# Second modulation moved from the LRU tiles into the S5 input and transform stages, and two LRU steps moved from VectorE to ScalarE

## The chip, the core and the metric

The kernel runs on one core of a Trainium2 chip. The metric is the device time of one execution in microseconds (us). Before the change it was 2331.53 us, the median of three runs (2328.48, 2331.53 and 2334.17).

The engines are called as the profile calls them: PE (TensorE, matrix multiply), DVE (VectorE), ACT (ScalarE), POOL (GpSimd) and SP (SyncE, which here issues nearly all transfers). Each runs its own queue strictly in order; a waiting instruction holds up everything behind it on its engine.

## What is computed

One layer of a hybrid backbone on 256 context tokens and 1024 latent tokens, width 1024, all in float32. Cut to what the change touches:

```python
m_lat = cond_lat @ w_mod[i] + b_mod[i]          # 1024 x 6144: six vectors of 1024
sh1l, sc1l, gt1l, sh2l, sc2l, gt2l = split(m_lat, 6)
z = modulate(rms_norm(h, norm1), sh1, sc1) @ w_in
xa, ga, zb, uc, zg = split(z)                   # LRU, its gate, RWKV, S5, merge gates

# LRU, each of two directions
xc = conv_centred(xa, conv_w, conv_b)           # bias + 4 taps
gate_r = sigmoid(xc @ w_a + b_a); gate_i = sigmoid(xc @ w_x + b_x)
log_a = -8 * gate_r * softplus(-lam)
a = exp(log_a)
u = sqrt(-expm1(2 * log_a)) * (gate_i * xc)     # the kernel uses a*a and tanh here
h = linear_scan(a, u)

# S5: input map, complex diagonal scan in both directions, output map, gate
# later: merge the branches with sigmoid(zg), w_out, gated residual (gt1l),
# norm and modulate with sh2l, sc2l, SwiGLU, gated residual (gt2l), last norm
```

`sh1l` and `sc1l` are the first modulation. The other four vectors (`gt1l`, `sh2l`, `sc2l`, `gt2l`) are the second modulation. They are first needed long after the mixers, in the output projection and the SwiGLU.

## The kernel before

The program is unrolled Python. The framework's scheduler puts each engine's instructions in an order of its own, from the order in which the code makes them and from its own estimate of when each can run. So the code gives the rough order, and the order that results has to be read from the built program.

Matrix products are split into high and low parts in a reduced float32 format: three products of `xh`, `xl` with `wh`, `wl` (for the merge gates `zh`, `zl`). One block of 128 output columns takes 24 matmuls for each piece of tokens: one of 256 and two of 512 with the context, two of 512 without. Each weight block is loaded by SP (`wr`, `zr`), copied to its high part by ACT and subtracted to its low part by DVE (`wl`, `zl`, L1296).

The stretch that matters is the first quarter, in this order:

- `front`: first norm and modulation. The S5 constants (`s5_setup`, some 250 small POOL operations) run beside it and after it.
- S5 input (`s5_u`): four column blocks of `w_in`, stored to memory and loaded again in another layout (`s5u`).
- S5 transforms (`s5_front`, four times, q = 0 to 3): DVE and POOL build the matrices (`s5bb` L418 to L423, `s5wt` L434 to L436), PE transposes them (L442), ACT evicts, PE makes the kernel matrix (L453, from `s` written by DVE at L448; DVE copies it out at L455), a row of it is fixed up (L458, L460), and PE multiplies the input (L467), which ACT and DVE write to the state `s5h` (L474 to L477).
- S5 scan (`s5_scan`): 34 steps of four POOL operations each (L498 to L501), 31 on 320 columns and three on 64, each needing the step before. It needs the whole of `s5h`.
- LRU (`lru_setup`, then `lru_tile` for j = 0 to 3): input projection, four convolution taps (L137 is the first, with the bias; L140 the other three), gate matmuls (L150), sigmoid and tanh on ACT, then for each of two directions `a` and tanh on ACT (L159, L160), the square of `a` on DVE (L162), products (L161, L163, L165), a square root on ACT (L164) and the scan on DVE (L168, L171, L173). POOL adds the directions (L176) and multiplies by the gate (L181); both stand between steps of the S5 scan in POOL's queue. The tile buffers are single, so tile j+1 waits for tile j.
- S5 carry (`s5_carry`, eight times, L522 and L523, DVE and some POOL), which needs the scan's end; then S5 back (`s5_back`, L562) and the S5 gate (`s5_out`, L609).

Two generators are mixed into this. `s.bg` holds the merge gates (`zg`, 24 blocks of 48 matmuls, L1309); `s.fill(n)` advances it by n pieces of three matmuls, and it fills PE's gaps. `mod2` computes the second modulation on DVE: 16 chunks, each of four transfers (`wm`, 256 KB, L1264, two buffers) and eight operations on 128 x 256 (`macc`, L1267 and L1269), two for each transfer. Then two small matmuls (L1273) and a copy (L1274) end the chunk, and only then can the next begin, as `macc` has one buffer. One step of the generator is one transfer and its two operations. The steps are given out by

```python
FU, FF, FL, FB, FS, FO, FX = 4, 25, 26, 5, (2, 2, 1, 4), 8, 12

def mix(gen, n, fills):
    for k in range(n):
        side(gen, 1)
        s.fill(fills * (k + 1) // n - fills * k // n)
```

so that before the change one step goes ahead of everything, 16 go beside the S5 inputs, 16 beside the transforms and 33 behind LRU tiles 0 to 2 (11 each, which is where the generator ends).

Of the kernel before, what the change touches and what calls it, by code (L numbers as in the profile page):

```python
# [9 lines left out]
F32 = mybir.dt.float32  # L10
F32R = mybir.dt.float32r
AF = mybir.ActivationFunctionType
# [4 lines left out]
P = 128  # L17
# [76 lines left out]
class LruMixin:  # L94
    def lru_setup(s, pool):
        nc = s.nc
        lam = s.pv("lam")
        t = pool.tile([P, 4, 8], F32, name="lru_t", tag="lru_t")
        e, y, y2, a = (t[:, k] for k in range(4))
        nc.scalar.activation(e, lam, AF.Abs)  # L100
        nc.scalar.activation(e, e, AF.Exp, scale=-1.0)
        nc.vector.tensor_scalar(y, e, 2.0, None, op0=ALU.add)
        nc.vector.reciprocal(y, y)
        nc.vector.tensor_tensor(y, y, e, op=ALU.mult)
        nc.vector.tensor_tensor(y2, y, y, op=ALU.mult)
        nc.vector.tensor_scalar(a, y2, 1.0 / 17.0, 1.0 / 15.0, op0=ALU.mult, op1=ALU.add)
        for n in (13, 11, 9, 7, 5, 3, 1):
            nc.vector.tensor_tensor(a, a, y2, op=ALU.mult)
            nc.vector.tensor_scalar(a, a, 1.0 / n, None, op0=ALU.add)
        nc.vector.tensor_tensor(a, a, y, op=ALU.mult)  # L110
        nc.vector.tensor_scalar(y2, lam, -1.0, 0.0, op0=ALU.mult, op1=ALU.max)
        nc.vector.scalar_tensor_tensor(a, a, 2.0, y2, op0=ALU.mult, op1=ALU.add)
        nc.vector.tensor_scalar(a, a, -8.0, None, op0=ALU.mult)
        s.lru_c8 = a
        s.lru_hb = pool.tile([P, 8], F32, name="lru_hb", tag="lru_hb")
        nc.vector.tensor_scalar(s.lru_hb, s.pv("bx"), 0.5, None, op0=ALU.mult)

    def lru_tile(s, j, pool):
# [15 lines left out]
        cw, cb = s.pv("conv_w"), s.pv("conv_b")  # L134
        for o, t0, n in ((0, 0, NCTX), (259, NCTX, NLAT)):
            x = xc[:, t0 : t0 + n]
            nc.vector.tensor_scalar(x, xap[:, o : o + n], cw[:, j : j + 1], cb[:, j : j + 1],  # L137
                                    op0=ALU.mult, op1=ALU.add)
            for k in range(1, 4):
                nc.vector.scalar_tensor_tensor(x, xap[:, o + k : o + k + n], cw[:, 4 * k + j : 4 * k + j + 1], x,  # L140
                                               op0=ALU.mult, op1=ALU.add)
        hs = []
        for d in range(2):
# [15 lines left out]
            nc.scalar.activation(a, gr, AF.Exp, scale=c8)  # L159
            nc.scalar.activation(th, gr, AF.Tanh, scale=c8)  # L160
            nc.vector.scalar_tensor_tensor(gi, gi, 1.0, xc, op0=ALU.add, op1=ALU.mult)  # L161
            nc.vector.tensor_tensor(gr, a, a, op=ALU.mult)  # L162
            nc.vector.scalar_tensor_tensor(th, gr, 1.0, th, op0=ALU.add, op1=ALU.mult)  # L163
            nc.scalar.activation(th, th, AF.Sqrt, scale=-0.25)  # L164
            nc.vector.tensor_tensor(gi, gi, th, op=ALU.mult)  # L165
# [946 lines left out]
class Kern(LruMixin, S5Mixin, RwkvMixin, ParamMixin, SplitMixin):  # L1112
# [641 lines left out]
    def run(s):  # L1754
# [8 lines left out]
        def cl(*names):  # L1763
            for n in names:
                live.pop(n).__exit__(None, None, None)

        def side(gen, n):
            for _ in itertools.islice(gen, n):
                pass
# [6 lines that stand above are left out]
# [32 lines left out]
        for q in range(4):  # L1808
            if q > 1:
                side(s.s5_u(q, s5e, s.in_wp(23 + q, (s.wp, s5e)[q % 2])), 3)  # L1810
            mix(mod2, 4, FU)
        cl("s5e", "s5t")
        s.params(2)
        s.rwkv_const(op("rc"))
# [1 line left out]
        s5g = op("s5g")  # L1816
        for q in range(4):
            s.s5_front(q, s5g)
            mix(mod2, 4, FF)
        s.s5_kout()  # L1820
        cl("s5g", "s5f")
        lp = op("lru")
        s.s5_scan(lp)
        s.lru_setup(lp)
        for j in range(4):
            s.lru_tile(j, lp)
            if j < 3:
                side(mod2, 11)
            s.fill(FL)
        for e in range(8):  # L1830
            s.s5_carry(e, m2)
# [150 lines left out]
```

## Time and profile before

| | |
|---|---|
| time, median of three runs | 2331.53 us |
| time of the profiled execution | 2331.55 us |
| its span, first to last instruction | 2329.8 us |
| PE busy | 2102.5 us (90%) |
| DVE busy | 1508.0 us (65%) |
| POOL busy | 986.0 us (42%) |
| ACT busy | 904.2 us (39%) |
| mean granted PE clock | 0.952 of full speed |

The shares are means over stages with different limits. PE is the busiest engine, but it is not so everywhere: in the page's 40 slices of 58 us DVE and POOL stand at 8 to 9 tenths in the sixth to eighth, where the LRU tiles and the S5 scan run. Busy PE time is the union of overlapping matmuls, so the time per matmul is better taken from a run of them than from the mean of one. "Idle before" in a row is time in which the engine had nothing running, with what ended it behind the arrow.

### The profile page before, as it was taken

The page shows a single profiled execution, that of the slowest core. Times are in us where ns is not written, and L with a number is a line of the kernel's source. Part 1 is how long each engine was busy: PE and PEld are TensorE (multiplying, and loading weights), DVE is VectorE, ACT ScalarE, POOL GpSimd, SP SyncE. Part 2 cuts the span into 40 slices and gives each one's busy share as a digit, 9 for nine tenths or more (in the row PEclk, how much of TensorE's full clock was granted, in tenths as well). Part 3 has the DMA queues.
Part 4 walks back from the last instruction along what each step waited for, and adds up shares of the span by engine and source line. Part 5 has one row for each costly group of instructions (what it writes and reads, how often), then busy time and mean ns, then how long its engine had stood idle before and what let it go on. Part 6 is the DMA issues. An engine that isn't in the chain of part 4 may idle for free.

```text
span 2329.8 us, 38390 instructions
## 1 busy us (share of the span) xinstructions
PE 2102.5 (90%) x14573; PEld 1675.7 (72%) x14573; DVE 1508.0 (65%) x2218; ACT 904.2 (39%) x1698; POOL 986.0 (42%) x1169
## 2 busy tenths in 40 slices
PE   5979988887899988898699999898999999989998
PEld 3868866665778877776467676676788888878886
DVE  5656698889566888899843366936855555543533
ACT  5313354423334645454533333416433323233431
POOL 3662389955323494856100122544644444300302
PEclk8989999998999999998699999998999999999999
DMA  6634322221663535445967777544222222274540
GB/s 254 168 110 115 90 66 83 82 84 64 143 174 89 161 111 140 125 136 142 246 181 173 171 191 183 167 158 136 81 77 86 77 86 77 68 276 151 165 149 36
DMA packets 360550, 307.26 MB, mean 132 GB/s; under 512 B 66023, under 2 KB 311982, under 8 KB 359342
## 3 DMA queue, kind: packets, MB, share of 16 engines
q1 hardware_dynamic: 356782, 293.27, 43.5%
q10 hardware_dynamic: 2880, 10.49, 1.2%
q8 instruction: 115, 1.88, 0.3%
q0 software_dynamic: 704, 1.05, 0.2%
q14 instruction: 69, 0.57, 0.1%
HBM read 219.03 MB, written 85.70 MB: 131 GB/s over the span
## 4 chain that ended last, share of the span: by engine, by line
PE 56%; DVE 19%; POOL 9%; DMA 7%; issue 5%; ACT 3%; SPq 1%; DVEq 0%; POOLq 0%; ACTq 0%
PE mm L1563 18%; PE mm L1718 10%; PE mm L1303 8%; PE mm L1309 7%; PE cg L1011 2%; PE cg L985 2%; PE cu L998 2%; DMA wm<-in_w_mod_dram 1%; DVE zl L1296 1%; PE cy L1026 1%; POOL s L214 1%; DVE s5ct L522 1%; PE aux L609 1%; DVE macc L1269 1%; DVE rn L748 1%
## 5 line engine op out<-in xcount | busy, mean ns | idle before, releaser
L1563 PE MATMUL mm<-q,wt 128*128 128x512 f32 x1584 | 376.6, 398 | 4.5 <-DVE q L1477 3.2
L1563 PEld LDWEIGHTS mm<-q,wt 128*128 128x128 f32 x1584 | 299.4, 189 | 77.5 <-DVE q L1477 3.6
L1718 PE MATMUL mm<-wk,hk 128*128 128x512 f32 x960 | 224.2, 396 | 0.0
L1303 PE MATMUL mm<-xh,wh 128*128 128x512 f32 (+1 forms) x576 | 214.4, 380 | 8.4 <-ACT ya L180 6.1
L1303 PE MATMUL mm<-xl,wh 128*128 128x512 f32 (+1 forms) x576 | 214.3, 379 | 1.2 <-DVE xl L1219 1.2
L1718 PEld LDWEIGHTS mm<-wk,hk 128*128 128x128 f32 x960 | 180.4, 188 | 43.6
L1309 PE MATMUL mm<-xh,zh 128*128 128x512 f32 x384 | 159.6, 416 | 10.0 <-ACT zge L1345 5.8
L1309 PE MATMUL mm<-xl,zh 128*128 128x512 f32 x384 | 159.5, 415 | 0.0
L1303 PE MATMUL mm<-xh,wl 128*128 128x512 f32 (+1 forms) x576 | 141.2, 383 | 8.8 <-DVE wl L1296 6.6
L1303 PEld LDWEIGHTS mm<-xh,wh 128*128 128x128 f32 x576 | 114.3, 199 | 28.6 <-ACT ya L180 6.9
L1671 DVE TENSOR_TENSOR wk<-wraw,wk 128x512 fp32r<-128x512 f32 x80 | 55.9, 707 | 111.3 <-ACT wk L1670 111.3
L1303 PEld LDWEIGHTS mm<-xl,wh 128*128 128x128 f32 x576 | 113.8, 197 | 19.4 <-DVE xl L1219 1.5
L1309 PE MATMUL mm<-byt,bwh 128*128 128x512 f32 x384 | 118.6, 428 | 7.9 <-ACT bwh L1295 2.9
L1303 PEld LDWEIGHTS mm<-xh,wl 128*128 128x128 f32 x576 | 102.9, 197 | 30.1 <-DVE wl L1296 8.2
L1309 PE MATMUL mm<-xh,zl 128*128 128x512 f32 x384 | 110.1, 423 | 15.3 <-DVE zl L1296 15.3
L1691 POOL TENSOR_TENSOR acc<-acc,ot 128x512 f32<-128x512 f32 x14 | 19.0, 1358 | 225.7 <-DVE ot L1689 225.2
L1015 DVE TENSOR_TENSOR x<-cg,pcend 64x256 f32<-64x256 f32 x152 | 63.9, 421 | 77.9 <-PE cg L1011 35.4
L1476 ACT ACTIVATE wt<-wT 128x512 fp32r<-128x512 f32 x88 | 55.1, 631 | 142.5 <-PE mm L1563 130.5
L1309 PEld LDWEIGHTS mm<-xh,zl 128*128 128x128 f32 x384 | 75.4, 202 | 35.2 <-DVE zl L1296 18.3
L1269 DVE SCALAR_TENSOR_TENSOR macc<-wm,cs,macc 128x256 f32<-128x256 f32 x112 | 84.6, 755 | 22.3 <-DMA wm<-in_w_mod_dram 19.8
L1477 DVE TENSOR_TENSOR wt<-wt 128x512 fp32r<-128x512 f32 x66 | 60.5, 918 | 59.4 <-ACT wt L1476 59.0
L1293 POOL CAST bwh<-bwr 128x512 fp32r<-128x512 f32 x16 | 10.0, 624 | 209.6 <-PE mm L1309 112.1
(421 smaller groups left out, 4865.3 us busy)
## 6 DMA issues: line engine op xcount, KB each, us to landing
wt<-in_w_ffn_in_dram SPq DMA_DIRECT2D x44, 512.0 KB
wraw<-in_w_ffn_out_dram SPq DMA_DIRECT2D x44, 512.0 KB
wm<-in_w_mod_dram SPq DMA_DIRECT2D x64, 256.0 KB
gyl<-gyl SPq DMA_DIRECT2D x32, 512.0 KB
wr<-in_w_in_dram SPq DMA_DIRECT2D x27, 512.0 KB
zr<-in_w_in_dram SPq DMA_DIRECT2D x24, 512.0 KB
sgd<-zge SPq DMA_DIRECT2D x48, 256.0 KB
bsg<-sgd SPq DMA_DIRECT2D x48, 256.0 KB
```

The source lines that it names most:

```text
L985: s.pe = nc.tensor.matmul(ps[32 * q : 32 * q + 32, 64 * p : 64 * p + 64], gy[:, 2 * p + par, c - cb, 0:32], st["x"][:, p, par, :], start=T ...
L998: s.pe = nc.tensor.matmul(ps[o : o + 32, 64 * p : 64 * p + 64], st["tt"][32 * q : 32 * q + 32, p, st["cc"], :], st["gs"][32 * q : 32 * q + ...
L1011: s.pe = nc.tensor.matmul(sn[64 * par : 64 * par + 64, 64 * p : 64 * p + 64], sd[:, st["cc"], 2 * p + par, :], st["x"][:, p, par, :], star ...
L1015: V.tensor_tensor(xn[0:64, :, par, :], sn[r].rearrange("p (a k) -> p a k", a=4), vb(s.pcend[r, d, :, st["c"]], 64), op=ALU.mult)
L1269: nc.vector.scalar_tensor_tensor(acc, wm[:, j], s.cs[:, k + j, 0:1], acc, op0=ALU.mult, op1=ALU.add)
L1303: s.nc.tensor.matmul(ps, w(k), a(k), start=n == 0, stop=n == len(seq) - 1)
L1309: s.nc.tensor.matmul(ps, w[:, k], a[:, k], start=n == 0, stop=n == len(seq) - 1)
L1476: s.nc.scalar.activation(hi, raw, AF.Copy)
L1477: (eng or s.nc.vector).tensor_tensor(lo, raw, hi, op=ALU.subtract)
L1563: nc.tensor.matmul(ps, w[:, k], a[:, k], start=n == 0, stop=n == len(seq) - 1)
L1671: V.tensor_tensor(hl[:, 1], raw, hl[:, 0], op=ALU.subtract)
L1718: nc.tensor.matmul(banks[t, n], a[:, tk], b, start=k == 0 and q == 0, stop=k == NF - 1 and q == 2)
```

## The change

The steps of `mod2` are doubled beside the S5 inputs and the S5 transforms (eight for each q instead of four, with the same number of fills), the rest is drained behind the last transform, and none are left behind the LRU tiles. In the LRU tile the square of `a` becomes a second exponential of the gate with twice the scale, on ACT, and the first tap with its bias becomes an ACT operation with scale and bias. A small tile with the doubled scale is new.

```diff
@@ lru_setup
         s.lru_c8 = a
+        s.lru_c16 = pool.tile([P, 8], F32, name="lru_c16", tag="lru_c16")
+        nc.vector.tensor_scalar(s.lru_c16, a, 2.0, None, op0=ALU.mult)
@@ lru_tile
-            nc.vector.tensor_scalar(x, xap[:, o : o + n], cw[:, j : j + 1], cb[:, j : j + 1],
-                                    op0=ALU.mult, op1=ALU.add)
+            nc.scalar.activation(x, xap[:, o : o + n], AF.Identity, scale=cw[:, j : j + 1], bias=cb[:, j : j + 1])
@@ lru_tile
-            nc.vector.tensor_tensor(gr, a, a, op=ALU.mult)
+            nc.scalar.activation(gr, gr, AF.Exp, scale=s.lru_c16[:, 4 * d + j : 4 * d + j + 1])
@@ run
-            mix(mod2, 4, FU)
+            mix(mod2, 8, FU)
@@ run
             s.s5_front(q, s5g)
-            mix(mod2, 4, FF)
+            mix(mod2, 8, FF)
         s.s5_kout()
+        side(mod2, 4)
@@ run
             s.lru_tile(j, lp)
-            if j < 3:
-                side(mod2, 11)
             s.fill(FL)
```

What this does to the queues is shown at three places. Between the two line numbers of an instruction there is one: L1264 before is L1265 after.

SP's queue just ahead of the first S5 load, before (`sgd` stores a finished gate piece, `zr` loads the next gate weights, `wm` is a chunk's transfer, `s5u` and `s5b` are the first transform's inputs):

```order
L1264 DMA wm_1499<-in_w_mod_dram 128x2x256
L1264 DMA wm_1525<-in_w_mod_dram 128x2x256
L1346 DMA sgd<-zge 128x512
L1264 DMA wm_1562<-in_w_mod_dram 128x2x256
L1264 DMA wm_1720<-in_w_mod_dram 128x2x256
L1346 DMA sgd<-zge 128x512
L1291 DMA zr<-in_w_in_dram 128x8x128
L402 DMA s5u<-u_60 128x1280
L414 DMA s5b<-in_s_b_re_dram 64x8x16 x2
```

And after:

```order
L1347 DMA sgd<-zge 128x512 x2
L1292 DMA zr<-in_w_in_dram 128x8x128
L1265 DMA wm_1342<-in_w_mod_dram 128x2x256
L1265 DMA wm_1349<-in_w_mod_dram 128x2x256
L1265 DMA wm_1358<-in_w_mod_dram 128x2x256
L1265 DMA wm_1554<-in_w_mod_dram 128x2x256
L1347 DMA sgd<-zge 128x512 x2
L1292 DMA zr<-in_w_in_dram 128x8x128
L1265 DMA wm_1574<-in_w_mod_dram 128x2x256
L403 DMA s5u<-u_60 128x1280
L415 DMA s5b<-in_s_b_re_dram 64x8x16 x2
```

The first transform's loads stand behind seven gate weight loads instead of four, with the stores of the units between, and behind the transfers of more chunks.

DVE's queue between the second and the third transform, before (L475 and L477 evict the state, L1274 ends the chunk before, `zl` is a gate weight's low part, L448 and L455 begin the next part of a transform):

```order
L1274 COPY mod2t<-aux 128x2
L1267 TENSOR_SCALAR macc<-wm_1805,cs 128x256
L475 COPY s5h<-aux 64x2x32
L1296 TENSOR_TENSOR zl<-zr,zh 128x1024
L1269 SCALAR_TENSOR_TENSOR macc<-wm_1805,cs,macc 128x256
L477 COPY s5h<-aux 64x3x32
L477 COPY s5h<-aux 64x2x32
L1269 SCALAR_TENSOR_TENSOR macc<-wm_1969,cs,macc 128x256 x2
L1269 SCALAR_TENSOR_TENSOR macc<-wm_1994,cs,macc 128x256 x2
L1269 SCALAR_TENSOR_TENSOR macc<-wm_2017,cs,macc 128x256 x2
L448 TENSOR_SCALAR s_41_936<-s_39_916 64x8x16 x2
L455 COPY s_40_935<-aux 128x2x128
```

The same place after (the first operation of the first chunk stands two rows ahead of this piece):

```order
L1270 SCALAR_TENSOR_TENSOR macc<-wm_1879,cs,macc 128x256
L478 COPY s5h<-aux 64x2x32
L1270 SCALAR_TENSOR_TENSOR macc<-wm_1892,cs,macc 128x256 x2
L1270 SCALAR_TENSOR_TENSOR macc<-wm_1908,cs,macc 128x256 x2
L1270 SCALAR_TENSOR_TENSOR macc<-wm_1922,cs,macc 128x256 x2
L1275 COPY mod2t<-aux 128x2
L1268 TENSOR_SCALAR macc<-wm_1940,cs 128x256
L1270 SCALAR_TENSOR_TENSOR macc<-wm_1940,cs,macc 128x256
L1270 SCALAR_TENSOR_TENSOR macc<-wm_2095,cs,macc 128x256 x2
L1270 SCALAR_TENSOR_TENSOR macc<-wm_2108,cs,macc 128x256 x2
L1270 SCALAR_TENSOR_TENSOR macc<-wm_2124,cs,macc 128x256 x2
L449 TENSOR_SCALAR s_41_936<-s_39_916 64x8x16 x2
```

Two whole chunks stand ahead of L448 (now L449) where one stood, and the second needs PE's matmuls of the first.

PE's queue in the fourth transform, before (L1303 is an input projection of LRU, filler here):

```order
L442 MATMUL aux<-ident,s5wt 128x128 x4
L1303 MATMUL mm<-xh,wl 128x256 x6
L442 MATMUL aux<-ident,s5wt 128x128 x8
L453 MATMUL aux<-s_41_936,s5wt 128x32 x16
L1303 MATMUL mm<-xh,wl 128x256
L1303 MATMUL mm<-xh,wh 128x512
L1303 MATMUL mm<-xl,wh 128x512
```

PE's queue from the second transform's end through the third, after (the fourth reads the same):

```order
L1304 MATMUL mm<-xh,wl 128x512 x3
L468 MATMUL aux<-s5u,s5wb 128x160 x8
L1274 MATMUL aux<-ones,macc 128x1 x4
L443 MATMUL aux<-ident,s5wt 128x128 x16
L454 MATMUL aux<-s_41_936,s5wt 128x32 x16
L459 MATMUL aux<-s_40_935,ident 16x128 x2
L468 MATMUL aux<-s5u,s5wb 128x160 x16
```

The filler has gone to earlier places: ahead of the first L442 (now L443) stand 321 gate matmuls where 176 stood. Up to the last L467 PE has 1101 matmuls where it had 1040, from there to the first L562 it has 921 where it had 958, and up to the first L609 it has 2237 in both.

## Rows read from the trace of the kernel before

**Rows 1.** The page's first part: busy time, share of the span, instructions.

```profile
PE 2102.5 (90%) x14573; PEld 1675.7 (72%) x14573; DVE 1508.0 (65%) x2218; ACT 904.2 (39%) x1698; POOL 986.0 (42%) x1169
```

**Rows 2.** Busy us of each engine by stretch, then clock, DMA share, GB/s.

```profile
78.00:171.00 93.00, 81.45 (x376) 66.35 (x374) 54.74 (x115) 16.36 (x19) 66.77 (x174) 0.96 0.55 153
171.00:274.00 103.00, 102.07 (x591) 88.93 (x592) 59.46 (x149) 42.82 (x82) 17.51 (x21) 0.94 0.38 101
274.00:491.00 217.00, 176.85 (x687) 132.82 (x686) 192.60 (x161) 94.31 (x112) 199.49 (x167) 0.91 0.27 85
491.00:587.00 96.00, 78.58 (x322) 60.92 (x320) 89.46 (x86) 36.97 (x44) 43.83 (x21) 0.93 0.22 62
587.00:640.00 53.00, 44.34 (x287) 40.98 (x288) 29.34 (x39) 18.51 (x20) 20.04 (x18) 0.90 0.66 141
```

**Rows 3.** Chain that ended last: start us, us, a run of gate matmuls.

```profile
181.81 4.88 PE mm L1309 x21
```

**Rows 4.** Timeline of DVE ahead of the first transform: start us, us, operation.

```profile
151.11 1.22 DVE L1296 TENSOR_TENSOR zl<-zr,zh 128x1024 fp32r<-128x1024 f32 x1
...
160.88 0.29 DVE L418 TENSOR_TENSOR s5bb<-s5b,s 128x128 f32<-128x128 f32 x1 [8.37 <-DMA s5b<-in_s_b_re_dram]
```

**Rows 5.** Timeline of DVE, the chunks behind the first and second transform.

```profile
197.08 1.11 DVE L1267 TENSOR_SCALAR macc<-wm,cs 128x256 f32<-128x256 f32 x1
...
204.06 1.01 DVE L1269 SCALAR_TENSOR_TENSOR macc<-wm,cs,macc 128x256 f32<-128x256 f32 x2 [0.77 <-DMA wm<-in_w_mod_dram]
206.30 0.46 DVE L448 TENSOR_SCALAR s<-s 64x128 f32<-64x128 f32 x2 [1.23 <-PE aux L453]
...
222.22 0.34 DVE L1267 TENSOR_SCALAR macc<-wm,cs 128x256 f32<-128x256 f32 x1
...
229.33 2.04 DVE L1269 SCALAR_TENSOR_TENSOR macc<-wm,cs,macc 128x256 f32<-128x256 f32 x4 [3.65 <-DMA wm<-in_w_mod_dram]
```

**Rows 6.** Waits of DVE from 171 to 274: us in total, times, longest.

```profile
DVE s L460 <- PE aux L458: 6.3, 1, 6.3
```

**Rows 7.** Timeline of POOL: starts of scan steps alone, beside macc, beside LRU operations.

```profile
274.51 1.23 POOL L498 TENSOR_TENSOR s5p<-s5h,s 128x320 f32<-128x320 f32 x1 [0.37 <-DVE s5h L477]
...
291.62 0.92 POOL L498 TENSOR_TENSOR s5p<-s5h,s 128x320 f32<-128x320 f32 x1
...
295.56 0.94 POOL L498 TENSOR_TENSOR s5p<-s5h,s 128x320 f32<-128x320 f32 x1
...
348.03 1.00 POOL L498 TENSOR_TENSOR s5p<-s5h,s 128x320 f32<-128x320 f32 x1
...
352.40 0.98 POOL L498 TENSOR_TENSOR s5p<-s5h,s 128x320 f32<-128x320 f32 x1
...
448.45 2.04 POOL L498 TENSOR_TENSOR s5p<-s5h,s 128x320 f32<-128x320 f32 x1
...
458.05 0.94 POOL L498 TENSOR_TENSOR s5p<-s5h,s 128x320 f32<-128x320 f32 x1
...
490.59 0.49 POOL L501 TENSOR_TENSOR s5h<-s5h,s5p 128x64 f32<-128x64 f32 x1
```

**Rows 8.** Groups of DVE from 274 to 491: count, busy us, mean ns, idle before.

```profile
L1269 DVE SCALAR_TENSOR_TENSOR macc<-wm,cs,macc 128x256 f32<-128x256 f32 x53 | 54.1, 1021 | 7.3 <-DMA wm<-in_w_mod_dram 6.4
...
L162 DVE TENSOR_TENSOR gr<-a 128x1280 f32<-128x1280 f32 x6 | 11.8, 1959 | 7.4 <-ACT th L160 4.6 <-ACT a L159 2.9
...
L1267 DVE TENSOR_SCALAR macc<-wm,cs 128x256 f32<-128x256 f32 x7 | 5.9, 847 | 0.0
...
L137 DVE TENSOR_SCALAR xc<-xap,pv 128x1024 f32<-128x1024 f32 x3 | 4.4, 1454 | 0.0
```

**Rows 9.** Waits from 274 to 490: POOL for a tile's end.

```profile
POOL gi L176 <- DVE gi L173: 8.2, 2, 5.5
```

**Rows 10.** The tile gr: ns min/median/max of ACT's exponential.

```profile
L159 ACT ACTIVATE a<-gr,lru_t x8: 1362/1368/1371, 302.8 to 538.9; 128x1280 f32<-128x1280 f32 x8
```

**Rows 11.** Groups of DVE from 491 to 587.

```profile
L162 DVE TENSOR_TENSOR gr<-a 128x1280 f32<-128x1280 f32 x2 | 3.0, 1485 | 0.0
```

## The prediction

> **What bounds the kernel now.** I read first the page's busy times, then a table of five stretches, then the rows in which one engine waits for another. TensorE is busy 2102.5 us of a span of 2329.8 us [rows 1]; from the table on, the question is where it is not. Of the 227 us in which it is not busy, the five stretches that the change touches hold 79 [rows 2]: 11.6 us in 78 to 171 (S5 input and S5 constants), 0.9 us in 171 to 274 (the four S5 transforms), 40.2 us in 274 to 491 (POOL runs the S5 scan beside LRU tiles 0 to 2), 17.4 us in 491 to 587 (S5 carry and LRU tile 3), 8.7 us in 587 to 640 (S5 back). So before 274 TensorE is nearly full, and it is full because the gate matmuls (zg, L1309) fill its gaps. From 274 to 491 two other engines set the pace: POOL is busy 199.5 us of 217 and VectorE 192.6 [rows 2]. S5 carry cannot begin before POOL's scan has ended, at 491, and from there VectorE sets the pace, busy 89.5 us of 96 [rows 2].
>
> The change touches both halves: it takes VectorE work out of the stretch that waits for POOL, and puts it into the stretch before, whose end starts POOL's scan. The end of the kernel moves by the sum, since from the first S5 gate matmul (L609) on all engines have the same instructions left, in nearly the same order.
>
> **A: the S5 transforms begin later.** SyncE's queue holds the first S5 load three zg weight loads later than before, and TensorE's order has 321 zg matmuls ahead of the first S5 transpose (L442) instead of 176. 145 matmuls at 4.88/21 = 0.232 us [rows 3] are 33.7 us. TensorE was idle for 11.6 us in 78 to 171, above all where VectorE reached a zl only at 151.11 and then waited 8.4 us for the first transform's load, until 160.88 [rows 2, 4]. The extra zg units fill that. I let them take 10 of the 11.6: **A = +24**, between +22 (all filled) and +34 (none).
>
> **B: each transform waits for one more modulation chunk.** A chunk is eight macc operations behind four loads. Between two transforms VectorE ran one chunk before; now it runs two, one behind the other, ahead of the two L448 with which the next step starts. A chunk took from 197.08 to 205.07, 8.0 us, and from 222.22 to 231.37, 9.1 us, and not 8 x 0.51, because its loads come two at a time [rows 5]. Three groups get a second chunk (the last one, behind the fourth transform, holds up less): 3 x 8 = 24 us. Off it goes what VectorE stood waiting anyway: 1.2 us per group for TensorE at L448 [rows 5], so 2.4 us, and in the last group 6.3 us at L460 [rows 6], where TensorE was working through filler that now stands earlier. **B = +15**; at least +4 (chunks of 8 x 0.51 = 4.1 us), at most +27 (9.1 us each, no slack). TensorE cannot use this time: in the new order the third and fourth transforms have no filler between their own matmuls. So POOL's scan starts at 274.5 + 39, about 313 [rows 7].
>
> **C: the S5 scan beside LRU.** A scan step is four POOL operations. Alone it took 295.56 - 291.62 = 3.94 us; beside macc operations 352.40 - 348.03 = 4.37 us; beside LRU's own long operations 458.05 - 448.45 = 9.60 us [rows 7]. POOL is slowed by the long ones, and hardly by macc, which itself takes 1.02 us there instead of 0.51 [rows 5, 8]. So the 60 macc that leave give POOL 60 x about 0.1 = 6 us: the step beside them was 0.43 us longer, with four to five of them in it. Of the squares six stand in the stretch, 11.8 us [rows 8]; they spare POOL between 0 and 11.8, and I take 7, nearer to all than to nothing because of the 9.60 us step. The three long first taps give 2 of at most 4.4 [rows 8]. POOL waited 8.2 us for the end of a tile [rows 9]; tiles end sooner, so I take 3 of that, as by the new order ten scan steps stand ahead of tile 0's sum, where eight stood. **C = -18**, between -8 and -35.
>
> The Trainium skill, on its page "SBUF — State Buffer", section "SBUF: two separate sides", says that a VectorE operation with two SBUF inputs and a GpSimd operation hold a shared port pair in turn, each for its whole length, and that the other blocks fully. By that rule each macc that leaves would give POOL its own length; that is the first rival below. The step of 4.37 us speaks against it.
>
> ScalarE takes over eight exponentials of 1.37 us [rows 10] and eight taps. It is busy 94 us of 217 [rows 2]; the new order has no more table loads than the old. The exponential stands in a tile's chain where VectorE's square stood, 1.37 us for 1.96 [rows 8, 10], and would cost POOL only if a tile were to end after its scan steps; I count it at nothing, with up to 1.4 us in each of eight half-tiles, 11 us, if that cover is gone.
>
> **D and E: after the scan.** From 491 VectorE is the pace, and loses two squares, 3.0 us [rows 11], the first taps of tile 3 and the last macc and modulation copies: **D = -6**, between -10 and -2. Behind the first S5 back matmul TensorE has, by the order, 24 input-projection matmuls less, 24 x 0.232 = 5.6 us; that stretch waits for loads too: **E = -2**, between -6 and 0.
>
> Sum: 24 + 15 - 18 - 6 - 2 = **+13 us**. Against the profiled execution, 2331.55 us (a span of 2329.8 and 1.75 us around it, and the median of the runs is 2331.53), this is **2344 us**. With each term moved inside its bounds, not all at once, this case reaches from +2 to +28.
>
> **Rivals.** First, the LRU stretch gives back more. If every macc held POOL up for its own 0.51 us [rows 5], C would be 60 x 0.51 = 31 instead of 6, so -43, and the sum -12: 2320 us. It decides from the point where C, D and E together pass A and B, 39 us. For it speaks that both engines are over 88% busy there; against it stands the 4.37 us step. Chance 0.12.
>
> Second, the front hides the move. VectorE is busy 114 us of the 196 from 78 to 274 [rows 2], so 60 more macc at 0.51, 31 us, would fit in its 82 idle ones. If the later transforms hide the second chunk and the 145 matmuls only change places with filler, what is left of A and B is the extra TensorE work ahead of the scan, 61 matmuls at 0.232 = 14 us, less 11.6 of idle: +3. Sum 3 - 18 - 6 - 2 = -23: 2308 us. Against it: all queues are in order, and both chunks stand in front of L448. Chance 0.15.
>
> Third, the front stalls fully: A +34, B +25 (the fourth transform without its gain, chunks at 9.1 us), sum +33: 2364 us. For it speaks that chunks, weight loads and gate stores share SyncE's one queue, and that VectorE waited up to 3.7 us for one chunk load at 229.33 [rows 5]. Chance 0.15.
>
> Fourth, gain and loss meet within 5 us: 2327 to 2336 us, chance 0.08. That the change does not do what it says I exclude: the new order has 125 of the 128 macc ahead of LRU's first VectorE tap.
>
> **How the numbers follow.** The forecast has 0.50, of which 0.07 lies within 0.2%. About 0.2%, 4.7 us, is what a measurement of this kernel can tell from no change. Faster: 0.12 + 0.15 = 0.27. Same: 0.07 + 0.08 = 0.15. Slower: 0.43 + 0.15 = 0.58. The range goes from 2315, which takes in the first rival and leaves out the second, to 2368, which takes in the third: 2 in 10 are left out with the second rival and the tails. The forecast's own range is 2334 to 2360.
>
> **What would show it.** In the new profile: the first transform's L418 (now L419) near 185 instead of 160.9; POOL's first scan step near 313 instead of 274.5; TensorE with 30 us or more of idle time in the third and fourth transforms; the scan from first step to last near 199 us instead of 216.6; macc at 0.5 us throughout; carry and tile 3 some 6 us shorter. The forecast is wrong on A and B if the scan starts before 295, and wrong on C if the scan takes under 185 us.

## The result, and the profile after

The change makes the kernel slower: 2363.03 us, the median of four runs (2361.43 to 2364.61), against 2330.01 us for the kernel before beside it (2328.08 to 2334.17). The ratio is 1.0136, with a 95% interval of 1.0121 to 1.0150. The forecast was 2344 us, 13 us more than before; it became 33 us more. The sign and the way were right, the size was not: most of what follows is about the 20 us between.

The page's first part (as [rows 1]) says little of it. TensorE has the same 14573 matmuls and 11 us more of busy time, some of it at a lower clock:

```profile
PE 2113.4 (89%) x14573; PEld 1690.4 (72%) x14573; DVE 1460.6 (62%) x2203; ACT 922.0 (39%) x1714; POOL 980.7 (42%) x1169
```

The stage edges say more. They are the times of single instructions in the two traces:

| edge | before | after | shift | of it in this stage |
|---|---|---|---|---|
| first S5 transform operation on DVE (L418, now L419) | 160.9 | 197.9 | +37.0 | +37.0 |
| first S5 scan step on POOL | 274.5 | 323.6 | +49.1 | +12.1 |
| last scan step's end | 491.1 | 532.6 | +41.5 | -7.6 |
| first S5 back matmul (L562, now L563) | 587.6 | 619.1 | +31.5 | -10.0 |
| first S5 gate matmul (L609, now L610) | 651.1 | 680.7 | +29.6 | -1.9 |
| end of the span | 2329.8 | 2361.8 | +32.0 | +2.4 |

The windows of the first two stages, before and then after (busy us of PE, weight loads, DVE, ACT, POOL; clock, DMA share, GB/s). Between the edges TensorE is idle 8.9 and 3.6 us before, 10.7 and 28.4 us after:

```profile
78.00:160.90 82.90, 74.03 (x343) 60.85 (x342) 45.84 (x102) 15.76 (x18) 61.39 (x170) 0.96 0.59 161
160.90:274.50 113.60, 110.00 (x627) 94.86 (x627) 68.81 (x165) 43.89 (x84) 23.04 (x24) 0.94 0.38 100
```

```profile
78.00:197.90 119.90, 109.23 (x507) 88.79 (x506) 63.22 (x138) 22.24 (x27) 63.43 (x171) 0.99 0.59 166
197.90:323.60 125.70, 97.26 (x528) 85.91 (x527) 77.81 (x189) 38.00 (x75) 24.88 (x25) 0.81 0.39 103
```

**Ahead of the transforms.** DVE's timeline after, which answers to [rows 4] (the bracket is the idle time before, with what ended it):

```profile
156.21 1.22 DVE L1297 TENSOR_TENSOR zl<-zr,zh 128x1024 fp32r<-128x1024 f32 x1
...
166.16 2.05 DVE L1270 SCALAR_TENSOR_TENSOR macc<-wm,cs,macc 128x256 f32<-128x256 f32 x4 [5.12 <-DMA wm<-in_w_mod_dram]
168.12 1.22 DVE L1297 TENSOR_TENSOR zl<-zr,zh 128x1024 fp32r<-128x1024 f32 x1
...
179.72 2.04 DVE L1270 SCALAR_TENSOR_TENSOR macc<-wm,cs,macc 128x256 f32<-128x256 f32 x4 [6.65 <-DMA wm<-in_w_mod_dram]
181.68 1.22 DVE L1297 TENSOR_TENSOR zl<-zr,zh 128x1024 fp32r<-128x1024 f32 x1
...
197.93 0.29 DVE L419 TENSOR_TENSOR s5bb<-s5b,s 128x128 f32<-128x128 f32 x1 [1.48 <-DMA s5b<-in_s_b_re_dram]
```

and SyncE's queue there (the second number is how long the group of issues took, waits within it included):

```profile
160.66 7.95 SPq L1265 DMA_DIRECT2D wm<-in_w_mod_dram  x4
168.70 5.00 SPq L1347 DMA_DIRECT2D sgd<-zge  x2
173.80 0.38 SPq L1292 DMA_DIRECT2D zr<-in_w_in_dram  x1
174.28 7.88 SPq L1265 DMA_DIRECT2D wm<-in_w_mod_dram  x4
182.21 7.07 SPq L1347 DMA_DIRECT2D sgd<-zge  x2
189.38 0.38 SPq L1292 DMA_DIRECT2D zr<-in_w_in_dram  x1
...
190.60 0.41 SPq L403 DMA_DIRECT2D s5u<-u  x1
```

A chunk and a gate unit take turns: four `wm` issues that take 8 us together (each waits for a buffer that macc has to free), two gate stores that wait for TensorE's unit, then the next gate weights, and only then the next chunk. One `zl` follows another after 11.9 and 13.6 us, where 48 gate matmuls at 0.232 us would be 11.1. The first S5 load, at 190.60, stands behind three more such turns.

**In the transforms.** TensorE's timeline after, second transform at full clock, then third and fourth:

```profile
247.90 3.66 PE L454 MATMUL aux<-s,s5wt 128*128 128x32 f32 x32
...
264.00 0.50 PE L1274 MATMUL aux<-ones,macc 128*128 128x1 f32 x4
273.82 0.98 PE L1274 MATMUL aux<-ones,macc 128*128 128x1 f32 x4 [9.32 <-DVE macc L1270]
274.67 3.65 PE L443 MATMUL aux<-ident,s5wt 128*128 128x128 f32 x16
278.11 6.88 PE L454 MATMUL aux<-s,s5wt 128*128 128x32 f32 x32
...
302.84 0.98 PE L1274 MATMUL aux<-ones,macc 128*128 128x1 f32 x4 [7.21 <-DVE macc L1270]
```

The second chunk's small matmul (L1274) stands ahead of the next transform's transposes in TensorE's queue, and nothing else stands between. So TensorE stands for 9.3 and 7.2 us until the chunk is summed. Behind each wait it runs with a granted clock of 0.61 to 0.72, mostly the lower of its two levels (1.2 GHz), and 32 matmuls of L454 take 6.88 us that took 3.66 us one transform earlier:

```profile
264.00:273.80 9.80, 0.51 (x6) 0.43 (x5) 7.21 (x20) 1.82 (x4) 2.34 (x2) 0.64 0.51 144
273.80:295.60 21.80, 19.64 (x92) 18.37 (x92) 13.01 (x31) 6.58 (x13) 2.74 (x2) 0.61 0.21 63
295.60:302.80 7.20, 0.04 (x1) 0.00 (x0) 4.78 (x13) 1.44 (x4) 0.00 (x0) 0.63 0.56 174
302.80:323.60 20.80, 17.07 (x95) 16.29 (x96) 9.24 (x29) 9.26 (x20) 3.10 (x9) 0.72 0.51 99
```

**The scan.** POOL's timeline after, first step, the sum of tile 0, last step (as [rows 7]), then POOL's wait (as [rows 9]):

```profile
323.60 1.01 POOL L499 TENSOR_TENSOR s5p<-s5h,s 128x320 f32<-128x320 f32 x1
...
385.76 2.38 POOL L177 TENSOR_TENSOR gi<-gi 128x1024 f32<-128x1024 f32 x1 [7.96 <-DVE gi L174]
...
532.20 0.42 POOL L502 TENSOR_TENSOR s5h<-s5h,s5p 128x64 f32<-128x64 f32 x1
```

```profile
POOL gi L177 <- DVE gi L174: 8.0, 1, 8.0
```

Tile 0's sum comes 62.2 us after the first step (332.23 - 274.51 = 57.7 before), and POOL waits as long for tiles as before, 8.0 us for 8.2. LRU starts later against the scan: its first gate matmul (L150, now L151) comes 25.7 us after the scan's first step, where it came 6.0 us after it before. In the ScalarE timeline a gate weight's copy stands ahead of tile 0's first sigmoid and waits 16.3 us for its load; in DVE's groups from 323.6 to 533 the tiles now wait for ScalarE:

```profile
350.92 1.06 ACT L1296 ACTIVATE zh<-zr 128x1024 fp32r<-128x1024 f32 x1 [16.27 <-DMA zr<-in_w_in_dram]
...
353.30 1.05 ACT L156 ACTIVATE gr<-aux,pv 128x256 f32<-128x256 f32 x2
```

```profile
L141 DVE SCALAR_TENSOR_TENSOR xc<-xap,pv,xc 128x256 f32<-128x256 f32 x12 | 11.9, 989 | 24.4 <-ACT xc L139 24.0
...
L164 DVE SCALAR_TENSOR_TENSOR th<-gr,th 128x1280 f32<-128x1280 f32 x6 | 11.0, 1839 | 21.3 <-ACT gr L163 21.3
```

### The profile page after: what moved, and what is told of

It reads as the page before. It is cut to its first block, busy times and chain, and to the rows that moved or that the text cites. A ratio compares the mean times of both kernels' runs of the same rounds, so it can differ in the third digit from the quotient of the medians.

```text
span 2361.8 us, 38411 instructions
## 1 busy us (share of the span) xinstructions
PE 2113.4 (89%) x14573; PEld 1690.4 (72%) x14573; DVE 1460.6 (62%) x2203; ACT 922.0 (39%) x1714; POOL 980.7 (42%) x1169
## 4 chain that ended last, share of the span: by engine, by line
PE 51%; DVE 9%; POOL 4%; DMA 4%; issue 3%; ACT 2%; SPq 0%; DVEq 0%; POOLq 0%; ACTq 0%
PE mm L1564 18%; PE mm L1719 10%; PE mm L1304 7%; PE mm L1310 5%; PE cg L1012 2%; PE cu L999 2%; PE cg L986 2%; PE cy L1027 1%; PE aux L610 1%; POOL nt L912 1%; POOL nt L910 1%; DVE rn L749 1%; PE aux L844 1%; DMA byr<-yd 1%; ACT aq L852 1%
## 5 line engine op out<-in xcount | busy, mean ns | idle before, releaser
L1304 PE MATMUL mm<-xh,wh 128*128 128x512 f32 (+1 forms) x576 | 219.3, 388 | 22.6 <-ACT ya L181 14.7
L1304 PEld LDWEIGHTS mm<-xh,wh 128*128 128x128 f32 x576 | 116.6, 203 | 43.4 <-ACT ya L181 15.7
L1304 PE MATMUL mm<-xh,wl 128*128 128x512 f32 (+1 forms) x576 | 135.0, 371 | 1.9 <-DVE wl L1297 1.0
L1310 PE MATMUL mm<-xh,zl 128*128 128x512 f32 x384 | 105.0, 410 | 3.2 <-DVE zl L1297 3.2
L1310 PEld LDWEIGHTS mm<-xh,zh 128*128 128x128 f32 x384 | 75.8, 198 | 34.9 <-ACT ya L181 10.0
L1003 ACT ACTIVATE x<-cu 32x256 f32<-32x256 f32 x156 | 58.5, 375 | 98.4 <-PE cu L999 95.5
```

The source lines that it names most:

```text
L1003: S.activation(st["x"][96:128, :, par, :], ps[o : o + 32, 0:256].rearrange("p (a k) -> p a k", a=4), AF.Copy)
L1304: s.nc.tensor.matmul(ps, w(k), a(k), start=n == 0, stop=n == len(seq) - 1)
L1310: s.nc.tensor.matmul(ps, w[:, k], a[:, k], start=n == 0, stop=n == len(seq) - 1)
```

## The experiments

Edges of all of them, in us, each from one profiled execution; times are medians, ratios are to the kernel before on the same chip, with the 95% interval. Kernels in which the code ahead of the scan is that of before, or nearly so, start the scan anywhere from 271.0 to 275.9, so a difference of two or three us between single edges tells little by itself:

| kernel | time | ratio | first S5 operation | scan starts | scan takes |
|---|---|---|---|---|---|
| before | 2330.0 | | 160.9 | 274.5 | 216.6 |
| the whole change | 2363.0 | 1.0136 (1.0121 to 1.0150) | 197.9 | 323.6 | 209.0 |
| act_only | 2319.0 | 0.9950 (0.9936 to 0.9965) | 159.8 | 272.8 | 208.0 |
| mod_only | 2381.0 | 1.0221 (1.0203 to 1.0239) | 197.7 | 322.3 | 215.8 |
| inputs_only | 2353.8 | 1.0101 (1.0086 to 1.0117) | 195.8 | 298.0 | 221.5 |
| transforms_only | 2352.7 | 1.0098 (1.0081 to 1.0114) | 160.7 | 295.6 | 224.5 |
| exp_only | 2318.3 | 0.9946 (0.9933 to 0.9959) | 161.0 | 271.0 | 212.1 |
| tap_only | 2331.6 | 1.0014 (1.0003 to 1.0026) | 161.0 | 274.5 | 215.1 |
| late | 2406.2 | 1.0322 (1.0307 to 1.0337) | 161.9 | 271.7 | 214.3 |
| act_late | 2388.0 | 1.0239 (1.0220 to 1.0257) | 163.5 | 275.9 | 207.3 |
| ff31 | 2374.2 | 1.0187 (1.0169 to 1.0205) | 197.3 | 327.1 | 210.5 |
| noload | 2335.5 | 1.0035 (1.0022 to 1.0048) | 174.2 | 291.3 | 211.2 |
| macc2 | 2348.6 | 1.0091 (1.0075 to 1.0107) | 181.1 | 307.0 | 208.7 |
| exp_macc2 | 2331.7 | 1.0015 (1.0002 to 1.0028) | 164.4 | 276.3 | 214.2 |

### The two halves of the change

The theory after the result was that the whole loss comes from the place of the modulation and that the ScalarE moves are nearly free; the rivals were that these moves eat the gain, and that they bring it. Four kernels take the change apart.

The ScalarE moves alone (against before):

```diff
-            nc.vector.tensor_scalar(x, xap[:, o : o + n], cw[:, j : j + 1], cb[:, j : j + 1],
-                                    op0=ALU.mult, op1=ALU.add)
+            nc.scalar.activation(x, xap[:, o : o + n], AF.Identity, scale=cw[:, j : j + 1], bias=cb[:, j : j + 1])
...
-            nc.vector.tensor_tensor(gr, a, a, op=ALU.mult)
+            nc.scalar.activation(gr, gr, AF.Exp, scale=s.lru_c16[:, 4 * d + j : 4 * d + j + 1])
```

> The kernel before with only the two ScalarE moves of the change (exponential for the square, first tap); the second modulation stays where it was. Theory 1 (the loss is all in the front, the ScalarE moves are nearly free): 2330 us, within 4 either way; POOL's scan from first step to last stays at 213 to 218 us (216.6 before). Theory 2 (the ScalarE moves lengthen the tiles, since VectorE in the changed kernel waits 25.6 us for the first taps and 21.3 us for the second exponentials, and so eat what the modulation gives): 2338 us or more, scan above 220 us. Theory 3 (these moves are what made carry and tile 3 shorter by 10 us): 2320 us.

Measured: 2319.0 us, 12.8 less than before, scan 208.0 us. The theory is wrong here and the third way right: these two moves are a gain of their own, and this kernel is faster than the one before and than the whole change. Its scan, first and last step, and POOL's one wait for a tile (3.3 us for 8.2 before):

```profile
272.80 0.93 POOL L499 TENSOR_TENSOR s5p<-s5h,s 128x320 f32<-128x320 f32 x1 [0.67 <-DVE s5h L478]
...
480.40 0.42 POOL L502 TENSOR_TENSOR s5h<-s5h,s5p 128x64 f32<-128x64 f32 x1
```

```profile
POOL gi L177 <- DVE gi L174: 3.3, 1, 3.3
```

The moved modulation alone (the whole change with those lines put back):

> The change with its two ScalarE moves undone: only the second modulation is moved. Theory 1: 2360 to 2366 us, scan beside LRU 207 to 212 us, start of the scan at 324. Theory 2: 2355 us or less, scan under 202 us. Theory 3: 2370 us or more, with the same start of the scan.

Measured: 2381.0 us, and the scan is 215.8 us, 0.8 less than before. So the move costs 49 us by itself, and the macc that leave the LRU stage make the scan hardly shorter. POOL's four operations of all 34 steps add up to 171.3 us instead of 177.6, but its waits grow by the same, from 10.6 us to 16.8:

```profile
POOL lru_bd L121 <- PE aux L150: 9.4, 1, 9.4
POOL gi L176 <- DVE gi L173: 7.4, 1, 7.4
```

The steps beside the S5 inputs alone:

```diff
-            mix(mod2, 4, FU)
+            mix(mod2, 8, FU)
...
             if j < 3:
-                side(mod2, 11)
+                side(mod2, 6)
```

> The kernel before with eight modulation steps beside each S5 input instead of four; four beside each transform as before, and the other steps still behind the LRU tiles (six, six and the rest). In the order 321 gate matmuls stand ahead of the first S5 transpose, as in the whole change (176 before). Theory 1 (three more gate units of some 12 us each stand ahead of the first S5 load, nothing absorbs them): first S5 operation at 198, scan from 311, time 2355 to 2363 us. Rival (the units only change places with filler of the transforms, which then run faster): first S5 operation at 198 too, but the scan from 290, time 2335 to 2342 us.

Measured: neither. The first S5 operation comes at 195.8, about as both expected, but the transforms then take 102.3 us instead of 113.6, as much of their filler has gone ahead of them; the scan starts at 298.0, 23.5 us later than before, and the time is 2353.8 us. The scan itself is 4.9 us longer, with POOL waiting 18.3 us in it for LRU. Up to the first S5 operation TensorE is idle for 6.9 us, against 8.9 before and 10.7 in the whole change, which has the same order there:

```profile
78.00:195.70 117.70, 110.82 (x513) 90.83 (x512) 62.46 (x138) 22.07 (x27) 64.58 (x172) 0.97 0.61 173
195.70:298.00 102.30, 88.17 (x515) 76.77 (x514) 66.28 (x162) 37.64 (x75) 24.78 (x25) 0.90 0.37 95
```

The steps beside the transforms alone:

```diff
             s.s5_front(q, s5g)
-            mix(mod2, 4, FF)
+            mix(mod2, 8, FF)
...
             if j < 3:
-                side(mod2, 11)
+                side(mod2, 6)
```

> The kernel before with eight modulation steps beside each S5 transform instead of four; the S5 inputs as before, the other steps still behind the LRU tiles. 176 gate matmuls stand ahead of the first S5 transpose, as before. Theory 1 (the second chunk in front of L448 costs 12 us, less 3 to 6 that the LRU stage gives back): scan from 285 to 288, time 2334 to 2340 us. Rival (the 12 us arise only because the filler was used up ahead of the transforms; here the filler is still there and hides the chunk): scan from 274 to 278, time 2322 to 2329 us.

Measured: worse than both expected. The transforms take 134.9 us, 21.3 more than before, although filler is left in them; in the groups between the first L448 of one transform and the next, 24.7 and 26.3 us have become 34.9 and 36.1. And the scan is longer, 224.5 us, since POOL waits 21.3 us in it (12.4 and 8.1 us in two waits for LRU's tiles) instead of 10.6: LRU's first gate matmul comes 18.3 us after the scan's first step instead of 6.0. Why it comes so late was not taken apart.

```profile
160.70:295.60 134.90, 122.47 (x675) 105.87 (x674) 81.29 (x189) 43.70 (x84) 22.79 (x23) 0.94 0.41 113
```

```profile
POOL lru_bd L121 <- PE aux L150: 12.4, 1, 12.4
POOL gi L176 <- DVE gi L173: 8.1, 1, 8.1
```

### Which of the two ScalarE moves

> The kernel before with the exponential for the square alone; the first tap stays on VectorE. The two ScalarE moves together gave 12.8 us. Theory 1 (the square is 1.96 us in each of eight half-tiles and stands in a tile's chain; the tap is short): 2319 to 2324 us, scan 208 to 212 us. Rival (the first tap, which lets a tile's convolution begin without VectorE, gives most): 2325 to 2331 us, scan above 212 us.

> The kernel before with the first convolution tap on ScalarE alone; the square stays on VectorE. The exponential alone gave 0.9946, both 0.9950. Theory 1 (the tap gives nothing or a loss: ScalarE waits for the padding and VectorE for ScalarE): 2328 to 2336 us, scan 215 to 219 us. Rival (each of the two gives the whole gain, since both only free VectorE): 2324 us or less, scan under 212 us.

Measured: the exponential alone gives all of it, 2318.3 us, and the tap alone nothing (2331.6 us, 1.0014). The theory holds for both, the exponential a little better than expected. It takes 14.8 us of squares off DVE (11.8 and 3.0, [rows 8, 11]), and the time is 13 us shorter, but that the one makes the other is not shown: of the 17.1 us between the two traced executions (exp_only's was its fastest) 4.5 are in the scan and 5.6 between its end and the first S5 back matmul, where the squares stood; 3.5 are ahead of the scan and 5.5 behind the S5 gate, where none did, and S5 back is 2.0 longer.

### What macc beside the scan costs, with the front unchanged

The second half of the modulation goes behind the S5 stage, as chunks of 128 columns:

```diff
-            if j < 3:
-                side(mod2, 11)
...
+        mod2 = s.mod2(op("m2b"), 2 * D, 4 * D, P)
         out = s.s5_out(op("s5o"))
         next(out)
-        s.fill(FO)
+        mix(mod2, 16, FO)
...
-        s.fill(FX)
+        mix(mod2, 48, FX)
```

> The kernel before with the second half of the second modulation (columns 2048 to 4095) computed beside the S5 output gate and the RWKV low-rank stage, in chunks of 128 columns, instead of behind the LRU tiles; the first half stays where it was, so TensorE's and VectorE's order up to the scan's start is that of before, and nearly no macc is left beside the scan. It measures what the macc beside LRU cost, with the front unchanged. Theory 1 (macc gives POOL back about 6 us in its steps, as in the whole change, and with the front unchanged the tiles keep their lead, so that the waits don't take it back): scan 207 to 212 us (216.6 before), time 2320 to 2328 us. Rival (POOL waits for the tiles in any case): scan 214 to 218 us, time 2328 us or more. A further way: the chunks delay the gate stage, 2335 us or more with a short scan.

> The same, with the two ScalarE moves of the change. Theory 1: both gains add up, the scan takes 198 to 204 us, time 2306 to 2314 us. Rival: the scan stays at 207 or 208 us as with the ScalarE moves alone, 2317 to 2323 us.

Measured: the scan takes 214.3 us without macc beside it (216.6 with), and 207.3 with the ScalarE moves (208.0 with both). The rival holds both times: without the 60 macc the scan is 2.3 and 0.7 us shorter, no more than edges differ anyway. The Trainium skill, page "SBUF — State Buffer", section "SBUF: two separate sides", has a VectorE operation with two SBUF inputs and a GpSimd operation block each other for a whole instruction; by that rule 60 macc of 0.51 us should have given some 30 us back (an estimate), and the runs speak against it. So does the trace of before, operation by operation: POOL's step operations on 320 columns take 0.95 us on average with nothing on VectorE beside them (6 of them) and 1.06 us beside macc alone (24). Steps and waits trade: without macc POOL waits 4.6 us instead of 10.6, but its step operations add up to 181.8 us instead of 177.6. That they then meet more of LRU's long operations is likely, but not shown.

The times, 2406 and 2388 us, come from the new place, as the further way had it, though the scan is not short: in late S5 back is 27 us longer than before, and what lies behind the S5 gate 58 us. TensorE meets there the same wait as in the transforms, 13 times (its waits from 571 to 820 us in late, then two windows with its clock, 0.73 and 0.70):

```profile
PE aux L1274 <- DVE macc L1270: 66.5, 13, 7.1
```

```profile
680.00:740.00 60.00, 25.97 (x116) 21.16 (x114) 29.14 (x82) 6.07 (x10) 0.00 (x0) 0.73 0.34 96
740.00:800.00 60.00, 32.40 (x147) 27.41 (x148) 31.70 (x61) 10.37 (x14) 10.50 (x25) 0.70 0.22 62
```

### What makes a chunk dear in the front

More filler beside the transforms of the whole change:

```diff
-            mix(mod2, 8, FF)
+            mix(mod2, 8, 31)
```

> The whole change with 31 instead of 25 fill pieces beside each S5 transform: 72 more gate matmuls (16.7 us at 0.232) stand ahead of the end of the transforms, most of them between the second and the third, where TensorE stood idle for 9.3 us behind the small modulation matmul and then ran at a lower clock. Theory 1 (idle TensorE and its lower clock in the third and fourth transform are what made the second chunk cost 24 us instead of 15): the scan starts at 318 to 325 us, not later than in the whole change (323.6) in spite of the extra matmuls, and the time is 2348 to 2358 us. Rival (the chunks' loads and sums set the pace, and extra matmuls only stand in the way): the scan starts at 332 to 340 us, time 2363 us or more.

Measured: the scan starts at 327.1, between the two: of 16.7 us of added matmuls 13 did not delay it, and TensorE's idle time in the transforms falls from 28.4 to 17.8 us. But the time rises to 2374 us. So idle TensorE in the transforms is there to be filled, and yet filling it doesn't pay: the scan doesn't start earlier. Where the 11 us are lost is only partly seen: from the scan's end to the S5 gate the traced execution is 3.2 us longer, and 8.8 us behind the gate, but it was also the slowest of its four, 6 us above their median. Why it loses is not settled.

Only one load for each chunk, in the whole change:

```diff
-                wm = pool.tile([P, 2, W], F32, name="wm2", tag="wm2", bufs=2)
...
+                if k == 0:
+                    wm = pool.tile([P, 2, W], F32, name="wm2", tag="wm2", bufs=2)
```

> The whole change with only the first of each chunk's four weight loads; its other sums take the same tile again, so the second modulation is not the reference's. All sums and small matmuls stay. In the order 257 gate matmuls stand ahead of the first S5 transpose (321 in the whole change). Theory 1 (the loads set a chunk's pace, 8 us for 8 sums of 0.51): the scan starts at 292 to 302 us (15 us by the 64 fewer gate matmuls, three times 3 to 4 by shorter chunks), time 2332 to 2342 us. Rival (the order alone counts, chunks stay at 8 us through the small matmul and the one buffer): scan from 308 us, time 2347 us or more.

Measured: 2335.5 us, the scan from 291.3; the theory holds, the scan starting a little earlier than it said. About half of the 32.3 us by which it starts earlier than in the whole change is the order alone, 64 gate matmuls or 14.8 us, so the run does not price the loads by themselves. A chunk's sums now run in one go (seven in 3.60 us), and although the first S5 transpose stands behind 81 more gate matmuls than before (18.8 us), the first S5 operation is only 13.3 us later: 5.5 us of the added matmuls were absorbed, and TensorE's idle time up to there is 4.5 us (8.9 before).

```profile
156.76 3.60 DVE L1271 SCALAR_TENSOR_TENSOR macc<-wm,cs,macc 128x256 f32<-128x256 f32 x7
...
174.19 0.29 DVE L419 TENSOR_TENSOR s5bb<-s5b,s 128x128 f32<-128x128 f32 x1 [1.55 <-DMA s5b<-in_s_b_re_dram]
```

```profile
78.00:174.20 96.20, 91.72 (x432) 76.22 (x431) 57.70 (x138) 18.72 (x22) 64.60 (x170) 0.96 0.46 124
174.20:291.00 116.80, 104.87 (x599) 91.78 (x598) 77.93 (x189) 41.35 (x80) 23.62 (x24) 0.91 0.30 77
```

Two macc buffers in the whole change, the loads halved to make room:

```diff
-            acc = pool.tile([P, W], F32, name="macc", tag="macc")
+            acc = pool.tile([P, W], F32, name="macc", tag="macc", bufs=2)
...
-                wm = pool.tile([P, 2, W], F32, name="wm2", tag="wm2", bufs=2)
+                    wm = pool.tile([P, 1, W], F32, name="wm2", tag="wm2", bufs=3)
```

> The whole change with two macc buffers instead of one; to stay in the same memory the weight buffers are three of 128 rows instead of two of 256 (the loads are halved and doubled in number). A chunk's first sum needs no longer wait for TensorE's small matmul of the chunk before. In the new order 228 gate matmuls stand ahead of the first S5 transpose (321 in the whole change, 176 before), and there is filler again between the matmuls of the third and most of the fourth transform. Theory 1 (the one macc buffer ties each chunk to TensorE's queue, and that is what stretches the front): 93 fewer gate matmuls are 22 us, the transforms lose most of the 23 us of the second chunks; the scan starts at 284 to 300 us (323.6 in the whole change, 274.5 before), time 2322 to 2342 us. Rival (VectorE's sums and the loads themselves are too many for the front): scan from 310 us or later, time 2350 us or more.

Measured: between the two, 2348.6 us and the scan from 307.0. The loss against before is 19.6 us instead of 33.0: some 13 us go with the single buffer and the order that it makes, and more than half stays. In noload, with another order, the scan starts 15.7 us earlier still, so much of the rest may be the loads'; as macc2 also doubles their number, that is not shown.

The same buffers without the moved modulation, with the exponential (the memory pool of the modulation is also closed and opened again ahead of S5 carry):

> The kernel before with the exponential for the square and two macc buffers (weight buffers as three of 128 rows), the modulation steps where they were before. Theory 1 (before, too, each chunk waits a little for the small matmul, behind which the transforms wait; and the exponential gives its 12 us): 2306 to 2316 us, scan from 268 to 274 us. Rival (with one chunk for each transform the buffer costs nothing, and twice as many loads cost a little): 2317 to 2324 us.

Measured: 2331.7 us, 13 us above exp_only; both ways were wrong. With one chunk for each transform the second buffer buys nothing, and something in these edits costs 13 us, perhaps the loads (in the front 64 of 128 KB for 32 of 256 KB): the first S5 operation is 3.4 us later and the scan 2.1 us longer. Which of the edits costs it was not taken apart.

## Why the prediction was wrong in size, by its own steps

Two steps failed: in A, the 10 us that idle TensorE time was to take (13.0 us too low), and in C, what macc and POOL's waits were to give back (10.4 us too much). The split into halves shows it best. For the ScalarE moves the terms of the prediction add up to about -13 us (squares 7, taps 2, and some 4 of D), and they measured -12.8. For the modulation they add up to about +26, and it measured +49.

- **A, forecast +24 for the start of the transforms, measured +37.0: failed.** The working had 145 gate matmuls of 0.232 us, 33.7 us, right (TensorE is busy 35.2 us more up to there), and then let idle TensorE time take 10 us of them. The reading of that idle time was wrong. Of the 11.6 us 2.7 lie behind the first S5 operation, and while VectorE waited 8.4 us for the first load, TensorE was busy. What it waited for up to there were one `zl` and macc, before:

```profile
PE mm L1309 <- DVE zl L1296: 5.1, 1, 5.1
PE aux L1273 <- DVE macc L1269: 3.8, 2, 3.6
```

The wait for `zl` was filled, but the added units brought others, after:

```profile
PE aux L1274 <- DVE macc L1270: 7.9, 6, 3.5
PE mm L1310 <- ACT zh L1296: 2.8, 2, 2.5
```

So TensorE was idle 8.9 us before, 10.7 us after and 6.9 us in inputs_only, and the operation came 37.0 and 34.9 us later, all of the 33.7 and more. Each added unit brings a chunk with it, and the chunk's loads, the unit's stores and the next weights take turns in SyncE's one queue. noload speaks for the loads having a part in it: without three of four, and in an order of its own, 18.8 us of added matmuls came out as 13.3.

- **B, forecast +15, measured +12.1 behind A's +37.0: right.** The chunk's price of 8 us was right: from inputs_only to the whole change the three groups from one L448 to the next, and from the last to the scan, grow by 8.1, 7.3 and 8.2 us, 23.4 in all transforms (in transforms_only, where filler is left, by 10.2, 9.8 and 3.4 against before). Of the slack that was taken off, 8.7 us, the 6.3 us wait at L460 is down to 1.2 us, in inputs_only too, as the filler that TensorE worked through there has left; the waits at L448 are not gone (6.5 us before, 7.8 after). In all the transforms gain 11.3 us by the filler's leaving (inputs_only). A and B together were +39 and measured +49.1.
- **TensorE can't use the time: nearly right.** It was idle 28.4 us in the four transforms, 23.8 of them in the third and fourth, where 30 us were named. Its lower granted clock behind each wait was not foreseen.
- **C, forecast -18, measured -7.6: failed.** The squares and taps (9 together) fit in sum: act_only has -8.6 with the macc in place. Their way was another, though: POOL's step operations there are only 3.1 us shorter, its waits 6.6 us (4.0 for 10.6), and the two moves alone give -4.5 and -1.5. The macc (6) and POOL's waits (3) are wrong: late has -2.3 with the front unchanged, mod_only -0.8. A tenth of a us was a fair price for a POOL operation beside macc (1.06 us for 0.95), but only 24 have macc alone beside them. And POOL's waits in the scan are 9.9 us for 10.6, as LRU's gate matmuls begin 25.7 us into the scan instead of 6.0, which the working did not have. In mod_only the steps do give back 6.3 us, and the waits take 6.2 of it.
- **ScalarE at nothing: not contradicted.** DVE waits 45 us for ScalarE in the tiles of the whole change, and the scan is shorter all the same.
- **D, forecast -6, measured -10.0; E, forecast -2, measured -1.9.** D is at the end of its bounds; from the scan's end to the first S5 back matmul act_only is 7.0 us shorter than before, mod_only 4.9. That E fits may be luck: the same stretch is 3.7 us longer in act_only and 3.5 in mod_only, and why is open. The last 2.4 us, behind the S5 gate, were not forecast.
- **The range.** Single terms moved inside their bounds don't give +2 to +28: C at -35 alone would give -4, and its terms at their most (6, 11.8, 4.4 and 8.2) add up to 30, not 35. The measured +33 lies outside of that reach.

Of the rivals the third, a front that stalls fully, gave 2364 us and came nearest to the time (2363.0), but in part by luck: its A of +34, nothing absorbed, is borne out (+37.0), while its B of +25 was 13 us too high, as the filler's leaving gave 11 back, and its C of -18 was 10 us too much; these errors nearly cancel. The first rival, that every macc holds POOL for its own length, is out by late and mod_only. The second, that the front hides the move, is out: each of the two S5 halves alone costs over 20 us.

What would have shown it ahead: the trace of before has the turns already, with TensorE waiting for `zl` and for macc in that stretch. The question to put to idle time is what ended it, and whether the added work brings that cause along.

## What to carry to other kernels

Work that is spread beside another stage must be priced with its loads and with its last step: here a small matmul behind a chain of sums and loads held up TensorE's whole queue (9.3 and 7.2 us, and 66.5 us in late) where no other work stood between two chunks. Idle time of an engine is no free place: ask first what ended it and which waits the added work brings along. And a change of several parts is worth taking apart: here one line, the square as a second exponential on ScalarE, gives 0.9946 (0.9933 to 0.9959) by itself, while the move beside it costs about four times that.

## What the runs showed of the hardware

Macc operations hardly lengthen POOL's scan steps, though they are lengthened themselves: macc takes 1.02 us beside the scan and 0.51 alone, while POOL's scan was at most 2.3 us shorter without 60 of them. LRU's long operations do lengthen the steps: in the trace of before POOL's operations on 320 columns take 1.7 to 2.2 us when they run mostly beside VectorE's products on 1280 columns, and as long as the linear scan when that is beside them:

```profile
453.64 3.48 DVE L168 TENSOR_TENSOR_SCAN gi<-a,gi 128x1280 f32<-128x1280 f32 x1
```

```profile
454.52 3.46 POOL L501 TENSOR_TENSOR s5h<-s5h,s5p 128x320 f32<-128x320 f32 x1
```

So it is the length of the operation beside it that counts in these rows, not the number of operations. How the two engines take turns is not shown. Taking away eight squares of up to 2 us, which stand in a tile's chain, went with 13 us, not all of them in the squares' own stages.
